# Eleven modulation vectors of a diffusion backbone: from scalar-times-column sums closed on TensorE to one fused multiply-and-sum per output tile on VectorE

## The chip, the cores and the metric

The kernel runs on one core of one Trainium2 chip, in float32 throughout. The metric is the device time of one launch in microseconds; three runs of the kernel before gave 1650.07, 1650.58 and 1651.04 us, so 1650.58 us is the median. One further execution was profiled.

## The reference

The reference is one inference step of a four-layer backbone over 128 context tokens and 256 latent tokens (384 columns in all) of width 1024. The two groups of tokens have different conditioning vectors, `c_ctx` and `c`. Each layer draws six modulation vectors of 1024 numbers from each condition:

```python
mod = jax.nn.silu(cond) @ p['w_mod'][i] + p['b_mod'][i]
sh1, sc1, g1, sh2, sc2, g2 = jnp.split(mod[:, None, :], 6, axis=-1)
h = x * (1 + sc1) + sh1
out = lru_mixer(h) or short_conv_mixer(h) or pool_mixer(h)      # by layer
x = layer_norm(ALPHA * x + g1 * out, ln_g[i, 0], ln_b[i, 0])
h = x * (1 + sc2) + sh2
f = squared_relu_mlp(h, w1, b1, w2, b2)                         # width 4096 inside
x = layer_norm(ALPHA * x + g2 * f, ln_g[i, 1], ln_b[i, 1])
```

So there are 4 x 6 modulation vectors, each a product of a 1024 x 1024 slice of `w_mod` with two condition vectors. Layers 0 and 3 have the recurrent mixer (LRU), layer 1 the short convolution, layer 2 the pooling.

## The kernel before, in words

**Layout.** Activations lie transposed: eight tiles `X0` to `X7` of 128 channels by 384 columns stay in SBUF for the whole run. A linear layer is cut into 128 x 128 weight tiles. Weights come from HBM in transfers of 16 tiles (1 MB, tile `raw`, four buffers). ScalarE copies 8 tiles (a half, 128 x 1024) to `whi` in the float32r type (L1289), and VectorE writes the remainder to `wlo` (L1295); `whi` and `wlo` have four buffers each (`W_BUFS`), and a half is split three halves ahead of its use (`LEAD`). TensorE then makes three products per weight tile, hi x hi, lo x hi and hi x lo (L197 to L199). One weight tile is one tick of a counter by which later work is deferred (`defer`, `tick`).

**The program's order.** The lines of the kernel trace instructions in one order; the framework then lists them anew, engine by engine, by its own idea of what is ready, and each engine works through its list in that order. Waits between engines are on semaphores. `tc.issue_after(x)` holds an instruction behind `x` on the same engine.

**Stages.** LRU of layer 0, its LayerNorm, the MLP of layer 0, its LayerNorm, and so on through four layers. An MLP is 512 weight tiles (64 halves): the first 16 hidden tiles up (`ORD_W1A`), their part of the down product, then the other 16 up and down. Each hidden tile costs VectorE two instructions (L832, L833), each down result two (L547). A LayerNorm after a mixer lets VectorE and GpSimd subtract a shift (L570) and gather sums of x and of its squares (`s1t` on GpSimd L594 and L597, `s2t` on VectorE L595 and L598 in the LRU layers), while TensorE still works on the last output tiles; then TensorE forms the means (L619 to L622).

**The modulation vectors.** The first two of layer 0 have a path of their own. Eleven (`ORD_MOD_PE`) are matrix-vector products on TensorE (`gemv`, L351). The other eleven (`ORD_MOD_DVE`) are made by VectorE during the MLPs of layers 0, 1 and 2, four, three and four of them, in `mac` (L426). For each of them:

- Four transfers of 1 MB bring the weights, with input channels on the partitions; the two buffers are a part of the scratch tile `scr` (shown as `mac`) and a tile `xs` of the same pool (shown as `macr`).
- VectorE multiplies a 128 x 512 piece by a per-partition scalar from `sil` and adds it to a 128 x 512 sum: 4 instructions of L444 (the first piece) and 28 of L446 per vector, for 2 halves of the output, 2 conditions and 8 input tiles. In all 44 and 308.
- The sum over partitions is closed on TensorE: `close` (L448) issues 8 small matmuls per half of a vector with the 0/1 columns `pick` as weights (L453), 22 times in all; then VectorE transposes the result from PSUM (L381) and adds the bias (L384). `finish` lets GpSimd form the combined scales from the vector.

The instructions of `mac` are deferred to ticks after the start of the MLP, spread by `step`.

Of the kernel before, what the change touches and what calls it, by code (L numbers as in the profile page):

```python
# [123 lines left out]
NSCR = 12 * LB  # L124
# [6 lines left out]
def backbone_kernel(ctx, tc, xT, par, wmod0, wmodp, wmodv, w1, w2, lin, lgate, lout, scin, scout, poolw, y_out, st_out):  # L131
# [132 lines left out]
    pick = cst(64, "pick")  # L264
# [160 lines left out]

    def mac(vecs, first, step):  # L426
        t = scr.tile([P, NSCR], F32, tag="scr", name=nm("mac"))
        raw = [t[:, :2048], scr.tile([P, 6 * LB], F32, tag="xs", name=nm("macr"))]
# [8 lines left out]
        def one(i, q, k):
            a = sums[i // 2 % 2][k]
            x = raw[i % 2][:, 512 * q : 512 * q + 512]
            c = 4 * (i % 2) + q  # L440
            w = sil[:, c, k : k + 1]
            with tc.issue_after(hcur["end"].ins):
                if c == 0:
                    vec.tensor_scalar(a, x, w, None, op0=ALU.mult)  # L444
                else:
                    vec.scalar_tensor_tensor(a, x, w, a, op0=ALU.mult, op1=ALU.add)  # L446

        def close(i):  # L448
            (l, v), h, _ = blocks[i]
            ps = acc()  # L450
            for k in range(2):
                for j in range(4):
                    pe.matmul(  # L453
                        ps[32 * j : 32 * j + 32, :P],
                        lhsT=pick[:, 32 * k : 32 * k + 32],
                        rhs=sums[i // 2 % 2][k][:, P * j : P * j + P],
                        start=(k == 0),
                        stop=(k == 1),
                        tile_position=(0, 32 * j),
                    )  # L460
# [918 lines left out]
def _layout(i):  # L1379
# [61 lines left out]
_INS = ["xT", "par", "wmod0", "wmodp", "wmodv", "w1", "w2", "lin", "lgate", "lout", "scin", "scout", "poolw"]  # L1441
# [30 lines left out]
```

## Time and profile before

| what | value |
|---|---|
| runs, median of three | 1650.58 us (1650.07 to 1651.04) |
| profiled execution, its own time | 1649.62 us |
| span of its trace | 1647.8 us |
| mean granted TensorE clock | 0.989 |
| TensorE busy | 1583.4 us (96%) |
| VectorE busy | 1188.8 us (72%) |
| ScalarE, GpSimd busy | 749.8 us (46%), 362.7 us (22%) |
| moved by DMA | 287.75 MB, 175 GB/s |

In the rows of the profile an instruction is given by its line, engine, operation and tiles (out<-in, with buffer numbers left out), then the count, the busy time and the mean duration of one, and the time that its engine sat idle before it with what ended that. A busy time of TensorE is not time at its peak, since matmuls are pipelined; starts tell more than durations there. The three MLPs in which `mac` works lie at about 190 to 450, 590 to 860 and 950 to 1220 us.

### The profile page before, as it was taken

To read this page: it belongs to the slowest core of one execution; us is meant where nothing else is said; L and a number is where in the kernel's file an instruction comes from. 1 tells how busy PE (TensorE), PEld (TensorE's weight loads), DVE (VectorE), ACT (ScalarE), POOL (GpSimd) and SP (SyncE) were. 2 spreads that over 40 slices of the span, in tenths; PEclk is the share of its full clock that TensorE was granted. 3 is DMA by queue.
4 is the path that set the end of the run, shared out by engine and by line. 5 is a ranking of instruction groups with operands and counts; after the bars stand their busy time and mean duration, and the time that the engine had idled before them with its cause. 6 is when DMAs were issued, how large, how long until landed. Compare 5 with 4: busy or idle time off the path is not lost.

```text
span 1647.8 us, 24431 instructions
## 1 busy us (share of the span) xinstructions
PE 1583.4 (96%) x9656; PEld 1501.8 (91%) x9656; DVE 1188.8 (72%) x1822; ACT 749.8 (46%) x1130; POOL 362.7 (22%) x445
## 2 busy tenths in 40 slices
PE   6999999999999999999997899999999999999996
PEld 5778899999999999999996599999988889999995
DVE  4789998886475569867746899688467997434544
ACT  3796642343253345324424553244259947423432
POOL 2114440002320146000055360000541134000043
PEclk9999999999999999999998999999999999999998
DMA  9677456556443535654543256546423344333321
GB/s 358 253 282 268 141 207 244 201 189 237 140 155 124 200 133 205 230 178 159 223 157 128 103 205 244 202 171 226 154 90 119 143 160 144 124 123 123 128 77 38
DMA packets 42162, 287.75 MB, mean 175 GB/s; under 512 B 4800, under 2 KB 6976, under 8 KB 8128
## 3 DMA queue, kind: packets, MB, share of 16 engines
q1 hardware_dynamic: 42048, 286.20, 48.4%
q8 instruction: 75, 1.23, 0.3%
q14 instruction: 39, 0.32, 0.1%
HBM read 284.59 MB, written 1.59 MB: 174 GB/s over the span
## 4 chain that ended last, share of the span: by engine, by line
PE 80%; DVE 12%; ACT 4%; issue 2%; POOL 1%; DMA 1%; SPq 0%; DVEq 0%; POOLq 0%; ACTq 0%
PE acc L197 26%; PE acc L199 25%; PE acc L198 25%; DVE wlo L1295 2%; DVE lru L879 1%; DMA raw<-in_wmod 1%; ACT hidf L930 1%; PE acc L453 1%; DVE X L570 1%; DVE hidf L958 1%; DVE X L547 1%; ACT L933 1%; ACT hidf L933 1%; DVE X L659 1%; POOL h L723 1%
## 5 line engine op out<-in xcount | busy, mean ns | idle before, releaser
L1295 DVE TENSOR_TENSOR wlo<-raw,whi 128x1024 fp32r<-128x1024 f32 x338 | 433.7, 1284 | 168.0 <-ACT whi L1289 166.7
L1289 ACT ACTIVATE whi<-raw 128x1024 fp32r<-128x1024 f32 x338 | 356.1, 1056 | 428.1 <-PE acc L199 351.7
L197 PE MATMUL acc<-h,whi 128*128 128x384 f32 (+2 forms) x1488 | 507.6, 341 | 16.0 <-ACT h L718 10.5
L198 PE MATMUL acc<-h,wlo 128*128 128x384 f32 (+2 forms) x1488 | 504.5, 339 | 0.0
L199 PE MATMUL acc<-h,whi 128*128 128x384 f32 (+2 forms) x1488 | 476.5, 340 | 3.1 <-POOL h L723 3.1
L197 PE MATMUL acc<-hid,whi 128*128 128x384 f32 (+1 forms) x1216 | 412.8, 340 | 0.8 <-ACT hid L975 0.8
L199 PE MATMUL acc<-hid,whi 128*128 128x384 f32 (+1 forms) x1216 | 409.4, 337 | 0.9 <-DVE hid L979 0.9
L198 PE MATMUL acc<-hid,wlo 128*128 128x384 f32 (+1 forms) x1216 | 409.2, 336 | 0.0
L197 PEld LDWEIGHTS acc<-h,whi 128*128 128x128 f32 x1488 | 280.9, 189 | 26.5 <-ACT h L718 11.6
L199 PEld LDWEIGHTS acc<-h,whi 128*128 128x128 f32 x1488 | 277.5, 188 | 6.7 <-POOL h L723 5.5
L198 PEld LDWEIGHTS acc<-h,wlo 128*128 128x128 f32 x1488 | 280.7, 189 | 1.6 <-issue 0.5
L197 PEld LDWEIGHTS acc<-hid,whi 128*128 128x128 f32 x1216 | 228.3, 188 | 5.2 <-issue 2.8
L199 PEld LDWEIGHTS acc<-hid,whi 128*128 128x128 f32 x1216 | 228.4, 188 | 1.5 <-DVE hid L979 1.5
L198 PEld LDWEIGHTS acc<-hid,wlo 128*128 128x128 f32 x1216 | 228.3, 188 | 0.9
L830 ACT ACTIVATE tmp<-acc,par 128x384 f32<-128x384 f32 x128 | 74.3, 580 | 259.1 <-PE acc L199 259.1
L570 POOL TENSOR_TENSOR X<-X,ssb 128x384 f32<-128x384 f32 x49 | 55.6, 1169 | 483.8 <-ACT ssb L568 483.8
L547 DVE SCALAR_TENSOR_TENSOR X<-acc,m,X 128x128 f32<-128x128 f32 (+1 forms) x176 | 64.7, 412 | 125.5 <-PE acc L199 123.7
L446 DVE SCALAR_TENSOR_TENSOR mac<-macr,sil,mac 128x512 f32<-128x512 f32 x176 | 126.2, 754 | 0.0
L832 DVE TENSOR_TENSOR tmp<-tmp 128x384 f32<-128x384 f32 x128 | 72.2, 564 | 65.8 <-ACT tmp L830 65.7
L446 DVE SCALAR_TENSOR_TENSOR mac<-mac,sil 128x512 f32<-128x512 f32 x132 | 95.2, 759 | 0.0
L777 POOL TENSOR_SCALAR X<-X,ag,xbb 128x128 f32<-128x128 f32 x64 | 94.8, 1495 | 0.4
L420 POOL TENSOR_SCALAR sc<-m 128x16 f32<-128x16 f32 x7 | 2.8, 403 | 328.6 <-DVE m L384 328.2
(194 smaller groups left out, 1310.6 us busy)
## 6 DMA issues: line engine op xcount, KB each, us to landing
raw<-in_w SPq DMA_DIRECT2D x128, 1024.0 KB, 4.8
raw<-in_wmodp SPq DMA_DIRECT2D x26, 1024.0 KB, 4.9
macr<-in_wmodv SPq DMA_DIRECT2D x22, 1024.0 KB, 5.3
mac<-in_wmodv SPq DMA_DIRECT2D x22, 1024.0 KB, 4.8
park<-in_wmodp SPq DMA_DIRECT2D x18, 1024.0 KB, 8.2
raw<-in_lin SPq DMA_DIRECT2D x16, 1024.0 KB, 5.1
raw<-in_scin SPq DMA_DIRECT2D x12, 1024.0 KB, 4.8
raw<-in_wmod SPq DMA_DIRECT2D x8, 1024.0 KB, 7.7
```

Of the source, the lines that this page charges most:

```text
L197: pe.matmul(ps, lhsT=hi, rhs=xhi, start=first, stop=False)
L198: pe.matmul(ps, lhsT=lo, rhs=xhi, start=False, stop=False)
L199: late = lambda: pe.matmul(ps, lhsT=hi, rhs=xlo, start=False, stop=last)
L446: vec.scalar_tensor_tensor(a, x, w, a, op0=ALU.mult, op1=ALU.add)
L547: vec.scalar_tensor_tensor(Xt[c][:, o : o + n], ps[:, a:b], col(g, c, k), Xt[c][:, o : o + n], op0=ALU.mult, op1=ALU.add)
L570: (vec if fast and i > 2 else gp).tensor_tensor(Xt[i], Xt[i], ssb, op=ALU.subtract)
L777: gp.tensor_scalar(Xt[c][:, a:b], Xt[c][:, a:b], col(g, c, k), col(xb, c, k), op0=ALU.mult, op1=ALU.add)
L830: act.activation(r, ps[:, :T], AF.Relu, bias=par_t[:, i : i + 1])
L832: vec.tensor_tensor(q, r, r, op=ALU.mult)
L933: act.activation(S["tau", c], S["tau", c], AF.Sqrt, scale=0.25)
L1289: act.activation(hi, raws[id(raw)][:, i * 1024 : (i + 1) * 1024], AF.Copy)
L1295: vec.tensor_tensor(lo, raws[id(raw)][:, i * 1024 : (i + 1) * 1024], hi.bitcast(F32), op=ALU.subtract)
```

## The change

The weights of the eleven vectors are laid out the other way round in HBM: an output channel on each partition, the 1024 input channels along the row. A block is now 128 partitions x two rows of 1024 (two output tiles), 1 MB as before, four blocks to a vector. One VectorE instruction multiplies a 128 x 1024 row block by a row of the condition, broadcast to all partitions (`silb`), and sums along the row into one column (`accum_out`): 4 per block, 16 per vector, 176 in all. The products are written to a scratch area `prod` that nobody reads. `close` only adds the bias to the 128 x 16 result, without TensorE; `pick`, the closing matmuls, the transposes and the `xs` buffer are gone (both weight buffers lie in `scr` now).

The row `silb` (128 x 2048: 1024 numbers for each of the two conditions) is made once, by a new function that is traced behind the LayerNorm of layer 0's mixer: a 1 MB transfer, a ScalarE tanh, and two VectorE instructions, all 128 x 2048. The arithmetic of the vectors is otherwise the same.

```diff
-NSCR = 12 * LB
+NSCR = 5 * D
...
+    def setup_rows(crow):
+        nc.sync.dma_start(silb, crow)
+        t = scr.tile([P, NSCR], F32, tag="scr", name=nm("sb"))[:, : 2 * D]
+        act.activation(t, silb, AF.Tanh, scale=0.5)
+        vec.tensor_scalar(t, t, 1.0, 0.5, op0=ALU.add, op1=ALU.mult)
+        vec.tensor_tensor(silb, t, silb, op=ALU.mult)
...
     def mac(vecs, first, step):
         t = scr.tile([P, NSCR], F32, tag="scr", name=nm("mac"))
-        raw = [t[:, :2048], scr.tile([P, 6 * LB], F32, tag="xs", name=nm("macr"))]
+        raw = [t[:, : 2 * D], t[:, 2 * D : 4 * D]]
+        prod = t[:, 4 * D : 5 * D]
...
             with tc.issue_after(hcur["end"].ins):
-                if c == 0:
-                    vec.tensor_scalar(a, x, w, None, op0=ALU.mult)
-                else:
-                    vec.scalar_tensor_tensor(a, x, w, a, op0=ALU.mult, op1=ALU.add)
+                vec.scalar_tensor_tensor(
+                    prod,
+                    raw[i % 2][:, D * q : D * q + D],
+                    1.0,
+                    silb[:, D * k : D * k + D],
+                    op0=ALU.mult,
+                    op1=ALU.mult,
+                    accum_out=rows[l, v][:, o : o + 1],
+                )
...
         def close(i):
-            (l, v), h, _ = blocks[i]
-            ps = acc()
-            for k in range(2):
-                for j in range(4):
-                    pe.matmul(
-                        ps[32 * j : 32 * j + 32, :P],
-                        lhsT=pick[:, 32 * k : 32 * k + 32],
-                        rhs=sums[i // 2 % 2][k][:, P * j : P * j + P],
...
-            collect(l, v, ps[:, :P], 4 * h)
-            if h == 1:
-                finish(l, v)
+            l, v = blocks[i][0]
+            m = modT[l, v] = rows[l, v]
+            o = PCOLS["bmod"][0] + (l * 6 + v) * 2 * C
+            vec.tensor_tensor(m, m, par_t[:, o : o + 2 * C], op=ALU.add)
+            finish(l, v)
...
     ln_tail(1, to_h(1, "mm"), use)
+    X(lambda: setup_rows(crow))
     use = mlp(0, ORD_MOD_DVE[0])
```

The change moves instructions in three places. Line numbers of the changed kernel are 2 to 3 higher from L549 on, and tile numbers differ because one constant tile is gone (`X_100` before is `X_99` now, both the fourth tile of x).

The first place is TensorE's list in the MLP of layer 0, where the first half vector is closed. Before:

```order
L197 MATMUL acc_2294<-h_1781,whi_2181 128x384
L198 MATMUL acc_2294<-h_1781,wlo_2182 128x384
L199 MATMUL acc_2294<-h_1781,whi_2181 128x384
L453 MATMUL acc_2318<-mac_1846,pick 32x128 x8
L197 MATMUL acc_2294<-h_1781,whi_2181 128x384
```

Now:

```order
L198 MATMUL acc_2287<-h_1778,wlo_2179 128x384
L199 MATMUL acc_2287<-h_1778,whi_2178 128x384
L197 MATMUL acc_2287<-h_1778,whi_2178 128x384
L198 MATMUL acc_2287<-h_1778,wlo_2179 128x384
L199 MATMUL acc_2287<-h_1778,whi_2178 128x384
```

The 22 groups of eight closing matmuls have left the list; every other matmul of the program stands in the order that it had.

The second place is VectorE's list in the LayerNorm of layer 0's mixer (`s2t` is the sum of squares, `X` the residual tiles as they take up the mixer's output). Before:

```order
L595 TENSOR_TENSOR s2t<-tmp_1563,tmp_1591 128x384
L1295 TENSOR_TENSOR wlo_1608<-raw_1341,whi_1607 128x1024
L598 TENSOR_TENSOR s2t<-s2t,tmp_1603 128x384
L547 SCALAR_TENSOR_TENSOR X_100<-acc_1491,m_857,X_100 128x128
L547 SCALAR_TENSOR_TENSOR X_100<-acc_1491,m_857,X_100 128x256
L1295 TENSOR_TENSOR wlo_1643<-raw_1341,whi_1642 128x1024
```

Now:

```order
L597 TENSOR_TENSOR s2t<-tmp_1560,tmp_1588 128x384
L1298 TENSOR_TENSOR wlo_1605<-raw_1338,whi_1604 128x1024
L600 TENSOR_TENSOR s2t<-s2t,tmp_1600 128x384
L429 TENSOR_TENSOR silb<-sb_1844,silb 128x2048
L549 SCALAR_TENSOR_TENSOR X_99<-acc_1488,m_854,X_99 128x128
L549 SCALAR_TENSOR_TENSOR X_99<-acc_1488,m_854,X_99 128x256
```

The second instruction of the `silb` setup has come in ahead of the fourth tile's residual. The first one (L428, 128 x 2048) stands 14 rows higher, behind the residual of the first tile and ahead of a `wlo`; on ScalarE the tanh stands right ahead of the `whi` of that same half.

The third place is VectorE's list in the MLP of layer 0, while the hidden tiles come up (`wlo` is a weight split, L832 and L833, now L834 and L835, finish a hidden tile). Before:

```order
L1295 TENSOR_TENSOR wlo_2223<-raw_1930,whi_2222 128x1024
L833 TENSOR_TENSOR hid_2209<-tmp_2208,hid_2209 128x384
L444 TENSOR_SCALAR mac_1846<-mac_1846,sil 128x512 x2
L446 SCALAR_TENSOR_TENSOR mac_1846<-mac_1846,sil 128x512
L832 TENSOR_TENSOR tmp_2246<-tmp_2245 128x384
L446 SCALAR_TENSOR_TENSOR mac_1846<-mac_1846,sil 128x512
L1295 TENSOR_TENSOR wlo_2261<-raw_1930,whi_2260 128x1024
```

Now:

```order
L1298 TENSOR_TENSOR wlo_2218<-raw_1931,whi_2217 128x1024
L450 SCALAR_TENSOR_TENSOR mac_1848,m_2005<-mac_1848,silb 128x1024
L834 TENSOR_TENSOR tmp_2241<-tmp_2240 128x384
L450 SCALAR_TENSOR_TENSOR mac_1848,m_2005<-mac_1848,silb 128x1024
L835 TENSOR_TENSOR hid_2242<-tmp_2241,hid_2242 128x384
L1298 TENSOR_TENSOR wlo_2255<-raw_1931,whi_2254 128x1024
L450 SCALAR_TENSOR_TENSOR mac_1848,m_2005<-mac_1848,silb 128x1024
```

Between two weight splits there stood three to four instructions of 512 elements, and now stand two of 1024. In the whole list 20 of the new instructions stand within the 12 splits of this stretch, 32 within the next 15 (the down product) and 12 within the 6 after that; before, 37 of the old ones stood within the first 12, and the last one came some 13 splits later than now. Of the 176 new instructions 50 stand right behind another one.

More of the change, by code (lines that the diff above doesn't have):

```diff
@@ L263, in backbone_kernel @@
     ssb = cst(T, "ssb")
-    pick = cst(64, "pick")
     Xt = [cst(T, f"X{c}") for c in range(C)]
@@ L293, in setup_params @@
         )
-        gp.memset(pick, 0.0)
-        gp.memset(pick[:, 0:1], 1.0)
-        gp.memset(pick[:, 33:34], 1.0)
         gp.memset(ones_s, 1.0 / P)
@@ L424, in finish @@
             comb["h", 2 * l + h] = (gg, bb)
+    silb = cst(2 * D, "silb")
+    def setup_rows(crow):
[4 more added lines that the diff above has]
+        vec.tensor_tensor(silb, t, silb, op=ALU.mult)
     def mac(vecs, first, step):
         t = scr.tile([P, NSCR], F32, tag="scr", name=nm("mac"))
-        raw = [t[:, :2048], scr.tile([P, 6 * LB], F32, tag="xs", name=nm("macr"))]
@@ L429, in mac @@
-        sums = [[t[:, 2048 + 1024 * i + 512 * k : 2560 + 1024 * i + 512 * k] for k in range(2)] for i in range(2)]
-        blocks = [(v, h, b) for v in vecs for h in range(2) for b in range(2)]
+        raw = [t[:, : 2 * D], t[:, 2 * D : 4 * D]]
+        prod = t[:, 4 * D : 5 * D]
+        blocks = [(v, b) for v in vecs for b in range(4)]
+        rows = {}
         def fetch(i):
             if i < len(blocks):
-                v, h, b = blocks[i]
-                nc.sync.dma_start(raw[i % 2][:, :2048], wmodv[MOD_DVE[v], h, b])
+                v, b = blocks[i]
+                nc.sync.dma_start(raw[i % 2], wmodv[MOD_DVE[v], b])
@@ L437, in one @@
         def one(i, q, k):
[L438 to L441, printed above, removed]
+            (l, v), b = blocks[i]
+            if (l, v) not in rows:
+                rows[l, v] = const.tile([P, 2 * C], F32, tag=f"m{l % 2}{v}", name=f"m{l}{v}")
+            o = 2 * (2 * b + q) + k
             with tc.issue_after(hcur["end"].ins):
-                if c == 0:
-                    vec.tensor_scalar(a, x, w, None, op0=ALU.mult)
-                else:
-                    vec.scalar_tensor_tensor(a, x, w, a, op0=ALU.mult, op1=ALU.add)
@@ L468, in mac @@
         for i in range(len(blocks)):
-            for q in range(4):
+            for q in range(2):
                 for k in range(2):
-                    defer(at(8 * i + 2 * q + k), lambda a=(i, q, k): one(*a))
+                    defer(at(8 * i + 4 * q + 2 * k), lambda a=(i, q, k): one(*a))
             defer(at(8 * i + 8) + 2, lambda i=i: fetch(i + 2))
-            if i % 2 == 1:
-                defer(at(8 * i + 8) + 10, lambda i=i: close(i))
+            if i % 4 == 3:
+                defer(at(8 * i + 8) + 4, lambda i=i: close(i))
     first_mod = const.tile([P, 32], F32, tag="m00", name="m00")
@@ L1417, in _layout @@
     r["wmodp"] = np.stack(wp).reshape(len(wp), 4, P, 2048)
-    wv = [wm[l, :, :, s].reshape(2, 4, P, 2, 4, 4, 32).transpose(3, 0, 2, 1, 5, 4, 6) for l, s in sum(ORD_MOD_DVE, [])]
-    r["wmodv"] = np.stack(wv).reshape(len(wv), 2, 2, P, 2048)
+    wt = a["w_mod"].reshape(DEPTH, D, 6, 4, 2, P)
+    wv = [wt[l, :, s].transpose(1, 3, 2, 0) for l, s in sum(ORD_MOD_DVE, [])]
+    r["wmodv"] = np.stack(wv).reshape(len(wv), 4, P, 2 * D)
+    crow = np.concatenate([a["c_ctx"], a["c"][0]])
+    r["crow"] = np.ascontiguousarray(np.broadcast_to(crow, (P, 2 * D)))
     w0 = wm[0, :, :, :2].reshape(2, 4, P, 2, 4, 2, 4, 32).transpose(4, 0, 2, 1, 6, 3, 5, 7)
@@ L1438, in _layout @@
     return r
[L1441 removed]
+_INS = ["xT", "par", "crow", "wmod0", "wmodp", "wmodv", "w1", "w2", "lin", "lgate", "lout", "scin", "scout", "poolw"]
 def _build(arrays):
```

6 lines of the change are left out of this document (1 added, 5 removed).

## The prediction

> **What bounds the kernel now.** I read the profile from the top: the engines' shares, then the chain that ended last, then the three MLPs, where the edited code works.
>
> ```profile
> PE 1583.4 (96%) x9656; PEld 1501.8 (91%) x9656; DVE 1188.8 (72%) x1822; ACT 749.8 (46%) x1130; POOL 362.7 (22%) x445
> PE 80%; DVE 12%; ACT 4%; issue 2%; POOL 1%; DMA 1%; SPq 0%; DVEq 0%; POOLq 0%; ACTq 0%
> ```
>
> TensorE (PE) carries 80% of the chain, VectorE (DVE) 12%. The windows of the three MLPs, in columns PE, PEld, DVE, ACT, POOL, clock, DMA share and GB/s:
>
> ```profile
> 190.00:450.00 260.00, 260.00 (x1580) 256.00 (x1580) 206.61 (x309) 100.75 (x143) 53.98 (x47) 1.00 0.57 203
> 590.00:860.00 270.00, 269.60 (x1658) 263.18 (x1657) 198.53 (x298) 108.38 (x160) 57.41 (x45) 1.00 0.51 183
> 950.00:1220.00 270.00, 269.14 (x1669) 262.17 (x1668) 208.00 (x311) 98.16 (x139) 56.96 (x71) 1.00 0.53 189
> ```
>
> PE never pauses there, at a granted clock of 1.00: whatever leaves its list shortens the run. But DVE is not far off. The same view in steps of 20 us:
>
> ```profile
> 210.00:230.00 20.00, 20.00 (x116) 20.00 (x115) 20.00 (x29) 9.57 (x15) 12.67 (x8) 1.00 0.60 211
> 250.00:270.00 20.00, 20.00 (x128) 19.55 (x127) 20.00 (x34) 6.15 (x7) 0.00 (x0) 1.00 0.63 225
> 270.00:290.00 20.00, 20.00 (x128) 19.55 (x127) 13.81 (x23) 5.31 (x5) 0.00 (x0) 1.00 0.71 250
> ```
>
> For some 75 us DVE is full as well and only just keeps pace. So two questions decide: what PE gets rid of, and whether DVE still keeps pace with the new instructions.
>
> **What PE loses.** The instructions of the closing line, and the chain of waits around the first close:
>
> ```profile
> L453 PE MATMUL acc<-mac,pick x352: 272/273/297, 231.2 to 1187.4; 128*32 128x128 f32 x176
> 231.13 0.17 PE acc L199
> 231.30 0.57 PE acc L453 x16
> 231.87 0.37 PE acc L197
> 232.24 0.17 PE acc L198
> ```
>
> Sixteen records make a close, 352 make 22. A close holds the chain for 0.57 us, and the matmul behind it for 0.37 instead of some 0.175 (0.17 or 0.18 in these rows), 0.195 more: 0.765 us together. All 22 lie in the MLPs, from 231.2 to 1187.4 us. The term is 22 x 0.765 = **-16.8 us**. Its lower bound is 22 x 0.57 = -12.5, were the pause behind a close an artefact of modelled ends.
>
> **What DVE has instead.** The groups by shape (busy us, mean ns) and a stretch of its timeline in the full phase:
>
> ```profile
> L446 DVE SCALAR_TENSOR_TENSOR mac<-macr,sil,mac 128x512 f32<-128x512 f32 x176 | 126.2, 754 | 0.0
> L446 DVE SCALAR_TENSOR_TENSOR mac<-mac,sil 128x512 f32<-128x512 f32 x132 | 95.2, 759 | 0.0
> L916 DVE SCALAR_TENSOR_TENSOR hidf<-hidf,lru 128x776 f32<-128x776 f32 x12 | 11.5, 961 | 3.4 <-ACT hidf L895 3.4
> L936 DVE TENSOR_TENSOR hidf<-hidf,hidf 128x776 f32<-128x776 f32 x10 | 9.4, 962 | 7.6 <-ACT hidf L933 7.6
> 252.82 0.56 DVE L832 TENSOR_TENSOR tmp<-tmp 128x384 f32<-128x384 f32 x1
> 253.29 1.22 DVE L1295 TENSOR_TENSOR wlo<-raw,whi 128x1024 fp32r<-128x1024 f32 x1
> 254.43 0.56 DVE L833 TENSOR_TENSOR hid<-tmp,hid 128x384 fp32r<-128x384 f32 x1
> 254.90 2.74 DVE L446 SCALAR_TENSOR_TENSOR mac<-macr,sil,mac 128x512 f32<-128x512 f32 x4
> 257.55 1.23 DVE L1295 TENSOR_TENSOR wlo<-raw,whi 128x1024 fp32r<-128x1024 f32 x1
> 258.68 2.08 DVE L446 SCALAR_TENSOR_TENSOR mac<-macr,sil,mac 128x512 f32<-128x512 f32 x3
> 260.67 0.74 DVE L547 SCALAR_TENSOR_TENSOR X<-acc,m,X 128x128 f32<-128x128 f32 x2
> 261.32 1.22 DVE L1295 TENSOR_TENSOR wlo<-raw,whi 128x1024 fp32r<-128x1024 f32 x1
> ```
>
> From start to start a split (`wlo`) takes 1.14 us, a hidden tile's instruction 0.47, a residual pair 0.65, an old sum 2.65/4 = 0.66. A scalar_tensor_tensor with an immediate scalar runs like a tensor_tensor (961 and 962 ns at 776 elements), so the new instruction over 1024 elements takes 1.14 us, as the split does. What is open is the sum that it must write out; no instruction of before does that. The nearest rows:
>
> ```profile
> 51.81 0.18 DVE L325 TENSOR_TENSOR sp<-sp 128x32 f32<-128x32 f32 x1
> 51.91 1.22 DVE L1295 TENSOR_TENSOR wlo<-raw,whi 128x1024 fp32r<-128x1024 f32 x1
> 48.38 1.33 DVE L319 SCALAR_TENSOR_TENSOR sp<-sp,sp 128x32 f32<-128x32 f32 x6
> ```
>
> A small instruction between others takes 0.10 us, one that depends on its forerunner 1.33/6 = 0.22. Lower bound: no time of its own, 1.14 in all. Upper: it starts when the duration of 1.22 has ended and takes a small one's 0.17, 1.39. I take 1.24 (the 0.10 row: its neighbours are other work), and 0.14 more, up to that upper end's 1.39, for the 50 of 176 that stand right behind another and wait for it: **1.28 us** on average, written t. In all, DVE then gives 176 x 1.28 = 225 us where it gave about 308 x 0.66 = 203 for L446, besides L444 and the transposes: little more work, but denser.
>
> [...]
>
> **Does DVE keep pace?** PE needs 24 x 0.175 = 4.2 us for a half of 8 weight tiles. Counting the MLP of layer 0 by its list in three stretches of 12, 15 and 6 splits, with 20, 32 and 12 new instructions:
> - 12 x 1.14 + 16 hidden tiles x 0.94 + 20t = 28.7 + 20t, against 50.4 us of PE
> - 15 x 1.14 + 7.5 residual pairs x 0.65 + 32t = 22.0 + 32t, against 63.0
> - 6 x (1.14 + 0.94) + 12t = 12.5 + 12t, against 25.2
>
> DVE falls behind by 64t - 75.4 us. How far may it? A split has four buffers, so ScalarE can start one (L1289) only as PE finishes the half four earlier, which is when it starts the half three earlier:
>
> ```profile
> 250.44 1.05 ACT L1289 ACTIVATE whi<-raw 128x1024 fp32r<-128x1024 f32 x1
> 263.31 1.06 ACT L1289 ACTIVATE whi<-raw 128x1024 fp32r<-128x1024 f32 x1 [3.92 <-PE acc L199]
> ```
>
> The half whose `whi` began at 250.44 is used from 263.31, the start of the third split after it; its `wlo` ended at 253.29 + 1.22 = 254.51. Cushion: 8.8 us. Before, 37 old sums stood in the first stretch: 28.7 + 37 x 0.66 = 53.1 against 50.4 + 0.8 for a close, so 1.9 us of it had gone already. The full cushion is 10.7, and PE waits only for t above (75.4 + 10.7)/64 = **1.35 us**. At 1.28 the lag is 6.5 and costs nothing; at 1.39 it is 2.9 over in each of the MLPs of layers 0 and 2. In layer 1, with 48 instructions in 25 splits by the same count, 48t - 57.3 - 10.7 is negative up to 1.41. Term: **0, up to +5.8**.
>
> **What the setup adds.** In the LayerNorm of layer 0's mixer DVE is full, and here PE does wait:
>
> ```profile
> 155.20 1.21 DVE L1295 TENSOR_TENSOR wlo<-raw,whi 128x1024 fp32r<-128x1024 f32 x1
> 156.87 4.90 DVE L570 TENSOR_TENSOR X<-X,ssb 128x384 f32<-128x384 f32 x5 [0.46 <-ACT ssb L568]
> 163.92 2.04 DVE L1295 TENSOR_TENSOR wlo<-raw,whi 128x1024 fp32r<-128x1024 f32 x1
> 166.35 0.73 DVE L547 SCALAR_TENSOR_TENSOR X<-acc,m,X 128x128 f32<-128x128 f32 x2
> 174.10 0.91 PE L619 MATMUL acc<-s1t,ones_m 128*128 128x384 f32 x2 [1.88 <-POOL s1t L597]
> ```
>
> The first DVE instruction of the setup (128 x 2048, one input) comes ahead of the 155.20 split; the old L444 took 483 ns for 512 by its group, so 1.3 (if fixed time is shared) to 1.9 us. The tanh on ScalarE, two splits' worth (2 x 1.06 at most), delays that split's `whi` by as much; 0.46 us of DVE idle hides a part. The subtractions behind it run beside GpSimd's (L570 at 0.98 each against 0.47 alone), so a later start wins some back: I take +0.3. The second (128 x 2048, two inputs) costs 2 x 1.07 + 0.07 = 2.2 us ahead of the 166.35 residual; the last sums of squares then come 2 to 2.5 us later. Some of that returns, since the shared last steps (sum, then residual of `X7`) overlap otherwise: **+2.0 us**, bounds 0.5 and 5 (all three at full length, nothing hidden). The transfer of `silb` takes the place that the first `macr` transfer had in SP's queue, 1 MB for 1 MB. The first transfer of `mac` now waits for the second setup instruction, and the weight transfer behind it for a split that is listed later still; it is needed only some 20 us on. GpSimd loses three small memsets, worth nothing.
>
> **Sum.** 1649.6 (profiled execution; the median of the runs is 1.0 higher) - 16.8 + 0 + 2.0 = 1634.8, on the scale of the runs up to 1635.8. I predict **1635.5 us**. Its own range: 1632 (no setup cost, 1649.6 - 16.8 = 1632.8, rounded out) to 1645 (the closes at -12.5 instead of -16.8 add 4.3 and the setup at 5 adds 3.0: 1642.8; with a part of the lag's 5.8).
>
> **Rivals.**
> - *The sum runs at half rate* (slower). With two fp32 inputs and a sum to keep, an element might take two steps: of the 1.14 us, 1.07 go with the elements (0.67 us between 384 and 1024 of them) and 0.07 are fixed, so t = 2 x 1.07 + 0.07 + 0.10 = 2.31. Lag over cushion: 64 x 2.31 - 86.1 = 62 us in two MLPs, 48 x 2.31 - 68.0 = 43 in one: 1635 + 167 = 1802 us. Against it: the same operation without a sum shows nothing of it (961 beside 962 ns). It decides from t = 1.35. [...] Chance 0.06.
> - *The write-out is dearer than any row says.* At t = 1.45 the MLPs lose 6.7 + 6.7 + 1.6 = 15 us: 1650, no change; at 1.5 some 24: 1659. For it: the chain of semaphores between neighbours; against: the 0.10 row. Chance 0.12.
> - *The setup stalls the LayerNorm* more than its lengths say (ScalarE and GpSimd queue behind it): +8 instead of 2, 1641. Chance 0.06.
> - *The closes were hidden*, and PE would have waited for weights or VectorE at those places: no change, 1650. Against it: no PE wait in the windows. Chance 0.04.
>
> **How the numbers follow.** The forecast has 0.72. A change of 0.2%, 3.3 us, is about what a measurement can tell here. Faster: 0.72 + 0.06 (setup) + 0.05 of the dear write-out = 0.83. Same: 0.04 + 0.04 of the write-out = 0.08. Slower: 0.06 + 0.03 = 0.09. Left out of 1632 to 1645 are the half rate, the hidden closes and most of the write-out, some 0.2.
>
> **What would show it.** In the profile after: no L453; PE without waits at L197 to L199 in the MLPs; L450 at 1.22 us, followed in 0.1 us or so by whatever reads the sum; a `wlo` that ends at least 3 us before its use; PE's wait ahead of the means at some 176 instead of 174.1 us. Wrong: PE idle in the MLPs with `wlo` as releaser, or L450 above 1.4 us.

## The result, and the profile after

| kernel | runs, median (us) | ratio to before, 95% interval |
|---|---|---|
| before | 1650.32 (1649.49 to 1651.04) | |
| changed | 1637.54 (1636.94 to 1638.17) | 0.9924 (0.9912 to 0.9936) |

The changed kernel is 12.8 us faster. 1635.5 us was predicted, 2.0 less than came. The profiled execution took 1636.94 us with a span of 1635.2, which is 12.6 less than before's span.

The shares of the engines on the page:

```profile
PE 1568.7 (96%) x9304; PEld 1496.4 (92%) x9304; DVE 1169.3 (72%) x1791; ACT 751.8 (46%) x1131; POOL 400.6 (24%) x442
```

The windows of the three MLPs, with the columns as before:

```profile
190.00:450.00 260.00, 260.00 (x1489) 259.63 (x1488) 203.65 (x303) 104.66 (x150) 72.45 (x51) 1.00 0.57 204
590.00:860.00 270.00, 269.60 (x1588) 265.87 (x1587) 194.49 (x290) 109.94 (x162) 72.77 (x47) 1.00 0.52 187
950.00:1220.00 270.00, 268.74 (x1574) 265.28 (x1573) 206.25 (x315) 106.97 (x157) 62.53 (x71) 1.00 0.52 185
```

TensorE is as full in the MLPs as it was, with the 352 records of the closes gone; the weight loads (second number) no longer have the gaps that the closes tore (259.63 of 260 against 256.00). VectorE stays full for longer, as windows of 20 us of the same kernel show:

```profile
250.00:270.00 20.00, 20.00 (x117) 20.00 (x116) 19.90 (x32) 6.10 (x8) 0.00 (x0) 1.00 0.78 266
310.00:330.00 20.00, 20.00 (x116) 20.00 (x115) 19.86 (x32) 7.08 (x9) 0.00 (x0) 1.00 0.77 278
330.00:350.00 20.00, 20.00 (x117) 20.00 (x116) 15.81 (x25) 8.99 (x14) 1.69 (x3) 1.00 0.64 232
```

Before, it had room again from 270 us; now only after 330. TensorE has 20.00 of 20 throughout.

The new instruction as a group (busy us, mean ns, idle time ahead):

```profile
L450 DVE SCALAR_TENSOR_TENSOR mac<-mac,silb 128x1024 f32<-128x1024 f32 x176 | 216.1, 1228 | 1.7
```

What it costs VectorE is read from its timeline, by starts (first number) more than by durations (second):

```profile
240.99 1.21 DVE L450 SCALAR_TENSOR_TENSOR mac<-mac,silb 128x1024 f32<-128x1024 f32 x1
242.14 0.08 DVE L450 DVE_READ_ACCUMULATOR mac<-mac,silb 128x1 f32 x1
242.25 1.23 DVE L450 SCALAR_TENSOR_TENSOR mac<-mac,silb 128x1024 f32<-128x1024 f32 x1
246.74 1.23 DVE L450 SCALAR_TENSOR_TENSOR mac<-mac,silb 128x1024 f32<-128x1024 f32 x1
247.89 0.08 DVE L450 DVE_READ_ACCUMULATOR mac<-mac,silb 128x1 f32 x1
247.89 0.56 DVE L834 TENSOR_TENSOR tmp<-tmp 128x384 f32<-128x384 f32 x1
257.56 1.22 DVE L1298 TENSOR_TENSOR wlo<-raw,whi 128x1024 fp32r<-128x1024 f32 x1
258.69 1.22 DVE L450 SCALAR_TENSOR_TENSOR mac<-mac,silb 128x1024 f32<-128x1024 f32 x1
```

The write-out of the sum is an instruction of its own (`DVE_READ_ACCUMULATOR`). Where another kind of instruction follows, that one starts at the same hundredth as the write-out: 246.74 to 247.89 is 1.15 us from start to start, as a split takes 1.13 (257.56 to 258.69). Where another of the new instructions follows, it starts 0.11 after the write-out: 240.99 to 242.25 is 1.26, and all 50 such pairs take 1.25 to 1.28. So t is 1.15 for 126 of the 176 and 1.26 for 50, 1.18 on average, not 1.28.

The LayerNorm of layer 0's mixer is where time was lost. TensorE's first pair of matmuls for the means:

```profile
175.85 1.65 PE L621 MATMUL acc<-s1t,ones_m 128*128 128x384 f32 x2 [5.13 <-POOL s1t L599]
```

The windows behind it, with the granted clock as the third number from the end:

```profile
176.00:178.00 2.00, 2.00 (x4) 1.09 (x5) 0.87 (x3) 0.52 (x1) 0.00 (x0) 0.50 1.01 422
178.00:180.00 2.00, 2.00 (x6) 0.99 (x4) 0.00 (x0) 0.35 (x1) 0.00 (x0) 0.74 0.49 201
```

TensorE waits 5.13 us for `s1t` where it waited 1.88 (GpSimd forms `s1t`, and in the chain of waits its last steps start behind VectorE's residuals, L549), and then works at a granted clock of 0.50, so that the pair of L621 takes 1.65 us instead of 0.91. Ahead of it VectorE has the setup in its timeline:

```profile
154.06 1.23 DVE L428 TENSOR_SCALAR sb<-sb 128x2048 f32<-128x2048 f32 x1 [0.25 <-ACT sb L427]
155.20 1.22 DVE L1298 TENSOR_TENSOR wlo<-raw,whi 128x1024 fp32r<-128x1024 f32 x1
156.34 4.89 DVE L572 TENSOR_TENSOR X<-X,ssb 128x384 f32<-128x384 f32 x5
165.81 2.28 DVE L429 TENSOR_TENSOR silb<-sb,silb 128x2048 f32<-128x2048 f32 x1
168.01 1.38 DVE L549 SCALAR_TENSOR_TENSOR X<-acc,m,X 128x128 f32<-128x128 f32 x4
```

**Where the 12.6 us went.** Spans carry some noise from the start: TensorE's first matmul started at 8.32 us here, and between 7.9 and 10.2 in the profiles of the experiments, each time behind a transfer of weights.

```profile
8.32 1.93 PE L489 MATMUL acc<-raw,sil 128*32 128x128 f32 x32 [8.32 <-DMA raw<-in_wmod]
```

So stages are compared by the starts of the means' matmuls (L619 before, L621 now) in TensorE's timeline, from one LayerNorm to another:

| stage, from means to means | before | changed | difference |
|---|---|---|---|
| start to the first means (layer 0's mixer) | 174.10 | 175.85 | +1.75 |
| MLP of layer 0 (with the rest of that LayerNorm) | 282.89 | 278.12 | -4.77 |
| mixer of layer 1 | 142.89 | 142.95 | +0.06 |
| MLP of layer 1 | 281.59 | 276.94 | -4.65 |
| mixer and MLP of layer 2 | 331.34 | 326.35 | -4.99 |
| all behind, to the end of the span | 435.0 | 435.0 | 0 |

The MLP of layer 1 had six closes: 0.775 us each. From the first means' start to the first matrix-vector products was 2.78 us before and is 4.34 now, by the lower clock; without these 1.56 the MLP of layer 0 has lost 6.33 us, 0.79 for each of eight closes. The first row is 3.25 us of longer wait, less 1.4 of an earlier start and 0.1 of small parts.

### The profile page after: what moved, and what is told of

Its sections match the earlier page's. It is cut to its first block, busy times and chain, and to the rows that moved or that the text cites. A ratio compares the mean times of both kernels' runs of the same rounds, so it can differ in the third digit from the quotient of the medians.

```text
span 1635.2 us, 23710 instructions
## 1 busy us (share of the span) xinstructions
PE 1568.7 (96%) x9304; PEld 1496.4 (92%) x9304; DVE 1169.3 (72%) x1791; ACT 751.8 (46%) x1131; POOL 400.6 (24%) x442
## 4 chain that ended last, share of the span: by engine, by line
PE 79%; DVE 12%; ACT 5%; issue 2%; POOL 1%; DMA 1%; SPq 0%; DVEq 0%; POOLq 0%; ACTq 0%
PE acc L199 26%; PE acc L198 26%; PE acc L197 25%; DVE wlo L1298 2%; DVE lru L881 1%; ACT hidf L932 1%; DMA raw<-in_wmod 1%; DVE hidf L960 1%; DVE X L549 1%; DVE X L572 1%; ACT L935 1%; ACT hidf L935 1%; DVE X L661 1%; DVE hidf L949 1%; POOL h L725 1%
## 5 line engine op out<-in xcount | busy, mean ns | idle before, releaser
L450 DVE SCALAR_TENSOR_TENSOR mac<-mac,silb 128x1024 f32<-128x1024 f32 x176 | 216.1, 1228 | 1.7
L832 ACT ACTIVATE tmp<-acc,par 128x384 f32<-128x384 f32 x128 | 74.2, 580 | 248.1 <-PE acc L199 248.1
L572 POOL TENSOR_TENSOR X<-X,ssb 128x384 f32<-128x384 f32 x49 | 56.1, 1179 | 488.7 <-ACT ssb L570 488.7
L834 DVE TENSOR_TENSOR tmp<-tmp 128x384 f32<-128x384 f32 x128 | 73.3, 572 | 104.2 <-ACT tmp L832 104.2
L549 DVE SCALAR_TENSOR_TENSOR X<-acc,m,X 128x128 f32<-128x128 f32 (+1 forms) x176 | 64.7, 411 | 113.9 <-PE acc L199 112.0
L779 POOL TENSOR_SCALAR X<-X,ag,xbb 128x128 f32<-128x128 f32 x64 | 126.9, 1997 | 0.4
L416 POOL TENSOR_SCALAR sc<-m 128x16 f32<-128x16 f32 x7 | 6.4, 911 | 270.8 <-DVE m L464 269.4
L835 DVE TENSOR_TENSOR hid<-tmp,hid 128x384 fp32r<-128x384 f32 x128 | 72.3, 565 | 0.3
```

Of the source, the lines that this page charges most:

```text
L450: vec.scalar_tensor_tensor(prod, raw[i % 2][:, D * q : D * q + D], 1.0, silb[:, D * k : D * k + D], op0=ALU.mult, op1=ALU.mult, accum_out= ...
L549: vec.scalar_tensor_tensor(Xt[c][:, o : o + n], ps[:, a:b], col(g, c, k), Xt[c][:, o : o + n], op0=ALU.mult, op1=ALU.add)
L572: (vec if fast and i > 2 else gp).tensor_tensor(Xt[i], Xt[i], ssb, op=ALU.subtract)
L779: gp.tensor_scalar(Xt[c][:, a:b], Xt[c][:, a:b], col(g, c, k), col(xb, c, k), op0=ALU.mult, op1=ALU.add)
L832: act.activation(r, ps[:, :T], AF.Relu, bias=par_t[:, i : i + 1])
L834: vec.tensor_tensor(q, r, r, op=ALU.mult)
```

## The experiments

All have the changed kernel or the kernel before as their base and were timed in five rounds. An undisturbed MLP of layer 0, at a full clock in its LayerNorm, takes 276.5 us from means to means in these traces; that is the measure for waits in it.

### The setup alone, in the kernel before

```diff
     ln_tail(1, to_h(1, "mm"), use)
+    X(lambda: setup_rows(crow))
```

> The kernel before, with the silb transfer and its three instructions added at the same place as in the changed kernel and silb left unused; everything else as before. Theory (the setup costs the LayerNorm 4.8 us, whatever the rest of the change does): 1650.3 + 4.8 = 1655.1 us, TensorE's wait ahead of the means about 5.1 us and a granted clock near 0.5 behind it. Prediction's term: 1652.3 us. Rival (the stall in the changed kernel comes from something else): 1650.3 us.

Measured: 1655.59 us, ratio 1.0034 (1.0021 to 1.0046), 5.4 us slower than the kernel before, timed beside it. TensorE's rows for the means:

```profile
177.02 1.65 PE L619 MATMUL acc<-s1t,ones_m 128*128 128x384 f32 x2 [5.13 <-POOL s1t L597]
178.46 1.49 PE L620 MATMUL acc<-s2t,ones_m 128*128 128x384 f32 x2
```

The same wait, to the hundredth, and the lower clock, with nothing else of the change in place. The setup costs 5 us here, not 2.

### The closes back, in the changed kernel

```diff
+    def idle_close():
+        ps = acc()
+        for k, j in [(k, j) for k in range(2) for j in range(4)]: pe.matmul(ps[32 * j : 32 * j + 32, :P], lhsT=ones_m[:, 32 * k : 32 * k + 32], rhs=ones_m, ...)
...
+            if i % 2 == 1: defer(at(8 * i + 8) + 10, idle_close)
```

> The changed kernel, with 22 groups of eight matmuls of the closing shape (128 x 32 weights, 128 columns, two passes over four row groups) put back on TensorE at the ticks of the old closes; they read a constant and nobody reads them, so they wait for no VectorE sum. Theory (each close held TensorE for 0.77 us by its own length and the pause behind it, and VectorE's new work costs nothing): 1637.5 + 17 = 1654.5 us. If the pause behind a close is an artefact of modelled ends: 1637.5 + 12.5 = 1650. Rival (the closes were dear because they waited for VectorE's sums, or because VectorE's lighter list made the rest run better): clearly below 1650.

Measured: 1655.29 us, ratio 1.0033 (1.0020 to 1.0045), 17.8 us more than the changed kernel. A group of the eight, in TensorE's timeline:

```profile
235.66 0.33 PE L199 MATMUL acc<-h,whi 128*128 128x384 f32 x1
235.92 0.65 PE L161 MATMUL acc<-ones_m 128*32 128x128 f32 x16
236.49 0.44 PE L197 MATMUL acc<-h,whi 128*128 128x384 f32 x1
236.77 0.33 PE L198 MATMUL acc<-h,wlo 128*128 128x384 f32 x1
```

0.57 us and a pause behind it, as in the closes of before, although these wait for no sum. The MLP of layer 1 takes 281.59 us from means to means, exactly what it took before. So the closes' price is TensorE's own, the pause behind them is real, and VectorE's new work costs the MLPs nothing. The rival of closes that were dear through their waits falls.

### The setup behind the LayerNorm

```diff
-        act.activation(t, silb, AF.Tanh, scale=0.5)
-        vec.tensor_scalar(t, t, 1.0, 0.5, op0=ALU.add, op1=ALU.mult)
-        vec.tensor_tensor(silb, t, silb, op=ALU.mult)
+        with tc.issue_after(hcur["mark_a"].ins): act.activation(t, silb, AF.Tanh, scale=0.5)
+        with tc.issue_after(hcur["end"].ins):
+            vec.tensor_scalar(t, t, 1.0, 0.5, op0=ALU.add, op1=ALU.mult)
+            vec.tensor_tensor(silb, t, silb, op=ALU.mult)
```

> The changed kernel, with the three instructions that make silb held behind the LayerNorm of layer 0's mixer (tanh behind the third tile's hi copy, the two VectorE instructions behind the tail's last one) instead of in its middle. Theory (the setup in the middle of the LayerNorm costs 4.8 us: 3.25 of longer TensorE wait ahead of the means, 5.13 against 1.88, and 1.6 of lower granted clock after it): about 1637.5 - 4.8 = 1632.7 us, TensorE's wait ahead of the means back at about 1.9 us, granted clock 1.00 at 172 to 180 us. Prediction's own term (2.0): 1635.5 us. Rival (the 4.8 us were the late start of something else, a transfer or the order of the residuals, and not the setup): 1637.5 us as now. If the setup only moves its cost into the start of the MLP (first splits late): also about 1637, but with a TensorE wait for wlo at 190 to 200 us.

Measured: 1635.41 us, ratio 0.9910 (0.9895 to 0.9925). The wait for the means and two later rows of TensorE:

```profile
173.86 0.91 PE L621 MATMUL acc<-s1t,ones_m 128*128 128x384 f32 x2 [1.91 <-POOL s1t L599]
191.68 0.44 PE L197 MATMUL acc<-h,whi 128*128 128x384 f32 x1 [1.57 <-ACT h L720]
197.51 0.97 PE L198 MATMUL acc<-h,wlo 128*128 128x384 f32 x4 [0.44 <-DVE wlo L1298]
```

ScalarE's timeline ahead of the first of those two:

```profile
188.01 1.28 ACT L427 ACT_TABLE_LOAD   x1
189.30 1.91 ACT L427 ACTIVATE sb<-silb 128x2048 f32<-128x2048 f32 x1
191.12 0.51 ACT L720 ACTIVATE h<-tmp 128x384 fp32r<-128x384 f32 x1
```

All of the 4.8 us in the LayerNorm come back (a wait of 1.91, the clock at 1.00), but more than half is lost again: the tanh needs a load of function tables here, 1.28 us, which it did not need beside the mixer, and the two hold up a copy of `h` that TensorE waits for. From means to means the MLP of layer 0 takes 279.34 us, 2.8 more than undisturbed. The theory on the LayerNorm holds; that the setup would be free right behind it does not, and the expected 1632.7 did not come.

### Only the second instruction behind the LayerNorm

```diff
-        vec.tensor_tensor(silb, t, silb, op=ALU.mult)
+        with tc.issue_after(hcur["end"].ins):
+            vec.tensor_tensor(silb, t, silb, op=ALU.mult)
```

> The changed kernel, with only the second VectorE instruction of the silb setup (2.28 us, two inputs) held behind the LayerNorm of layer 0's mixer; the tanh and the first VectorE instruction stay in it. It shows which of the two made TensorE's wait ahead of the means 3.25 us longer. By the prediction's two terms (the first +0.3, the second +1.7): the wait falls from 5.13 to about 2.2 us, with the clock at 1.00 behind it, and the run to about 1633.5 us (3 us of wait and 1.6 of clock less, perhaps 0.5 given back at the start of the MLP). Rival (the first and the tanh in front of it, ahead of the shift of the tiles, cost most): the wait stays above 4 us and the run at about 1637.

Measured: 1634.74 us, ratio 0.9910 (0.9896 to 0.9923). TensorE's rows for the means:

```profile
174.50 0.91 PE L621 MATMUL acc<-s1t,ones_m 128*128 128x384 f32 x2 [2.81 <-POOL s1t L599]
175.25 0.85 PE L622 MATMUL acc<-s2t,ones_m 128*128 128x384 f32 x2
175.90 1.49 PE L623 MATMUL acc<-X,ones_m 128*128 128x384 f32 x2
```

The second instruction was worth 5.13 - 2.81 = 2.32 us of wait, its whole length; the tanh and the first are worth 2.81 - 1.88 = 0.93. The clock fell all the same, in the middle of the four pairs (the third takes 1.49 us, 0.81 before), which was not expected behind a wait of 2.81.

### TensorE kept busy in its wait

```diff
+            if idx == 1: es = ExitStack(); es.enter_context(tc.issue_after(lastmm[0].ins)); [pe.matmul(m2[:, :P], lhsT=ones_m, rhs=ones_m, start=True, stop=True) for _ in range(NWARM)]; es.close()
```

(`NWARM` is 24; `lastmm` is the last product of the mixer.)

> The changed kernel, with 24 matmuls of 128 x 128 constants put on TensorE between the last output matmul of layer 0's mixer and the matmuls that form its means, in the place where TensorE now waits 5.1 us; their results are overwritten. Theory (the lower granted clock after that wait, 0.50 and 0.74, comes from the idle time and costs 1.6 us by itself): about 1636 us, the clock 1.00 at 176 to 180 us, the means still waiting for s1t at the same time. Rival (the clock falls there for another reason, or the 1.6 us are not on the path): 1637.5 us or a little more, with the lower clock still there.

Measured: 1636.60 us (1634.11 to 1638.87), ratio 0.9919 (0.9905 to 0.9932). TensorE's timeline, with the added matmuls (L620):

```profile
169.63 5.52 PE L620 MATMUL acc<-ones_m 128*128 128x128 f32 x48
174.99 0.84 PE L621 MATMUL acc<-s1t,ones_m 128*128 128x384 f32 x2
175.66 0.81 PE L622 MATMUL acc<-s2t,ones_m 128*128 128x384 f32 x2
```

The clock stays at 1.00 and the stage from the means through the MLP takes 276.47 us instead of 278.12. In this trace the lower clock went with the idle time; the runs alone, 0.9 us apart with wide spreads, would not show it.

### The setup in halves, among the first tiles of the MLP

```diff
+    def setup_half(p, s):
+        with tc.issue_after(hcur["last_a"].ins): act.activation(p, s, AF.Tanh, scale=0.5)
+        with tc.issue_after(hcur["end"].ins):
+            vec.tensor_scalar(p, p, 1.0, 0.5, op0=ALU.add, op1=ALU.mult)
+            vec.tensor_tensor(s, p, s, op=ALU.mult)
...
+        for k in range(2 if vecs is ORD_MOD_DVE[0] else 0): defer(10 + 8 * k, lambda k=k: setup_half(prod, silb[:, D * k : D * k + D]))
```

> The changed kernel, with the silb setup cut into two halves of 1024 (one per condition) that use the product area as scratch and stand behind the LayerNorm, among the first weight tiles of the MLP of layer 0, where VectorE is not full. Theory (the setup costs nothing where VectorE and ScalarE have room): TensorE's wait ahead of the means 1.9 us, none above 0.5 us in the first 20 us of the MLP, about 1632.7 us, 2.7 less than the version that held the whole setup right behind the LayerNorm (1635.4, with waits of 1.57 for h and 0.44 for wlo at 191 to 198 us). Rival (the tanh behind the LayerNorm costs ScalarE a change of function tables, so h or the hidden tiles come late again): 1634 to 1636 us with waits for ScalarE at 185 to 205 us.

Measured: 1633.10 us (1631.45 to 1634.71), ratio 0.9897 (0.9883 to 0.9910), the best median. TensorE waits 1.88 us for the means and nowhere for the setup; the load of tables (1.28 us, at 196.09) falls where ScalarE has room. But here too the clock fell, to 0.50, behind a wait of only 1.88:

```profile
173.40 0.91 PE L621 MATMUL acc<-s1t,ones_m 128*128 128x384 f32 x2 [1.88 <-POOL s1t L599]
174.15 0.95 PE L622 MATMUL acc<-s2t,ones_m 128*128 128x384 f32 x2
174.90 1.48 PE L623 MATMUL acc<-X,ones_m 128*128 128x384 f32 x2
```

### The same, with TensorE kept busy in the wait that is left

The two edits together, with `NWARM` 8.

> The version with the silb setup in halves in the MLP (1633.1 us), with 8 matmuls of constants (0.23 us each, 1.84 us) in TensorE's remaining wait of 1.88 us ahead of the means. Its profile had a granted clock of 0.50 behind that wait, which cost 1.4 us between the means and the matrix-vector products (4.19 us against 2.78). If the idle time brings the lower clock: 1.00 throughout, 1632 us. If the lower clock comes from elsewhere: 1633, with the clock still down.

Measured: 1633.25 us (1632.64 to 1633.49), ratio 0.9898 (0.9884 to 0.9912). In the profile the clock is 1.00 at this place and the MLP of layer 0 takes 276.57 us from means to means, against 277.98 in the version without. The medians are the same. What the trace shows at one place, 1.4 us, is within the scatter of the runs. Behind the same wait of 1.88 us the kernel before kept its clock at 1.00, so the version without need not have the fall in every execution; the last section shows what decides it.

### Longer new instructions, freely ordered

```diff
-NSCR = 5 * D
+NSCR = 5 * D + 512; EXT = 512
...
-                    raw[i % 2][:, D * q : D * q + D],
+                    raw[i % 2][:, D * q - EXT * q : D * q + D + EXT * (1 - q)],
```

> The changed kernel, with each of the 176 new instructions running over 1280 elements instead of 1024 (the sums take in 256 products too many), so that from start to start one takes about 1.15 + 256 x 1.07/1024 = 1.42 us. By the prediction's cushion (TensorE waits from t = 1.35; lag 64t - 86.1 in the MLPs of layers 0 and 2, 48t - 68.0 in layer 1): 4.8 + 4.8 + 0.2 = +9.8, 1647.3 us, with TensorE waits for wlo in the MLPs. Rival (the cushion is larger, since VectorE's list can be rearranged and the lag is made up between the stretches): 1637.5 us, no such waits.

> The same with 1536 elements (512 too many): t about 1.15 + 512 x 1.07/1024 = 1.69 us. By the prediction's cushion: 64 x 1.69 - 86.1 = 22 in each of two MLPs and 48 x 1.69 - 68.0 = 13 in one, +57, so 1695 us. Rival (larger cushion): if 256 costs nothing, then clearly less than 57; the difference between the two lengths gives the slope (64 + 64 + 48 instructions by 0.27 us = 47 us once VectorE sets the pace).

Measured: 1639.21 us (ratio 0.9934, 0.9921 to 0.9946) and 1637.59 us (0.9929, 0.9916 to 0.9941): nothing beyond 1.7 us, which is within the scatter, where 10 and 57 us had been expected. The instructions are as long as meant, here in the group of those with 1536 elements:

```profile
L450 DVE SCALAR_TENSOR_TENSOR mac<-mac,silb 128x1536 f32<-128x1536 f32 x176 | 309.4, 1758 | 0.8
```

VectorE is full until 390 us in that kernel, and TensorE is full beside it, as its windows show:

```profile
350.00:370.00 20.00, 20.00 (x116) 20.00 (x116) 20.00 (x29) 8.71 (x15) 0.00 (x0) 1.00 0.68 245
370.00:390.00 20.00, 20.00 (x116) 20.00 (x115) 20.00 (x29) 8.81 (x14) 0.00 (x0) 1.00 0.61 220
```

The reason stands in VectorE's list. The 64 new instructions of the first MLP span 32 weight splits in the changed kernel, 40 at 1280 elements and 47 at 1536. The framework that lists the instructions anew thus goes by their lengths: the longer they are, the fewer it puts between two splits. The prediction's lag was counted on a fixed list.

### The same instructions, packed into 32 splits

To hold the list fixed, two of them are put between each two splits in the MLPs of layers 0 and 2, 32 times, and a split is held behind those ahead of it. In layer 1, with 48 of them, the list was not fixed: they still span 24, 29 and 31 splits at the three lengths.

```diff
-            X(lambda: mac(todo, 32, 13.2 / len(todo)))
+            X(lambda: mac(todo, 32, 8.0 / len(todo)))
...
-        with after("mark_v"):
+        with after("mark_v"), after("stt"):
```

> The changed kernel, with the new instructions packed into the first 32 weight splits after the start of an MLP: exactly two between two splits in the MLPs of layers 0 and 2 (three in two gaps in layer 1), each split held behind the instructions ahead of it. Instructions as they are (1024 elements, t = 1.15). By the prediction's way of counting (12 splits of the up product with 16 hidden tiles, 16 of the down product, 4 up again) VectorE falls behind by 24t - 21.7 = 5.9 us in the first part and makes it up in the second, under the cushion of 10.7: no TensorE wait, 1637.5 us. Rival (there is hardly a cushion; the changed kernel is only fast because its list was spread to what VectorE can do): TensorE waits for wlo in the first part, up to 6 us in each MLP, up to 1650.

> The same packing with 1280 elements (sums with 256 products too many), t = 1.42 us. Lag by the prediction's counting: 24t - 21.7 = 12.4, then 32t - 43.8 = 1.6, then 8t - 8.5 = 2.9: 16.9 in all, 6.2 over the cushion of 10.7 in each of the MLPs of layers 0 and 2, nothing in layer 1: 1637.5 + 12.4 = 1650 us, with TensorE waits for wlo. Without a cushion 34 us: 1671. Rival (the order never matters, VectorE always catches up): 1637.5.

> The same packing with 1536 elements (512 products too many), t = 1.69 us. Lag by the prediction's counting: 18.9 + 10.3 + 5.0 = 34.2 us, 23.5 over the cushion in two MLPs, nothing in layer 1: 1637.5 + 47 = 1684 us. The freely ordered kernel with the same instructions took 1637.6, so what is over that is due to the order alone. Rival (order of no matter): 1637.5.

| elements | run (us) | ratio | MLP of layer 0 | of layer 1 | mixer and MLP of layer 2 |
|---|---|---|---|---|---|
| 1024 | 1638.97 | 0.9934 (0.9921 to 0.9946) | +0.5 | 0 | -0.3 |
| 1280 | 1655.92 | 1.0036 (1.0023 to 1.0049) | +9.3 | 0 | +8.0 |
| 1536 | 1694.40 | 1.0267 (1.0253 to 1.0281) | +26.7 | +2.1 | +26.4 |

The last three columns are the stages from means to means, against 276.5, 276.94 and 325.4 us (the last as in the freely ordered kernel with 1280 elements), those of layer 0 without the lower clock in its LayerNorm. The two longer ones came 6 and 10 us above what was expected, so the rival of an order that never matters falls. At 1536 elements the same work costs 57 us more than in a free order. A window of that kernel:

```profile
250.00:270.00 20.00, 15.71 (x85) 14.65 (x86) 20.00 (x27) 8.07 (x12) 1.25 (x1) 1.00 0.53 174
```

One of TensorE's waits in it:

```profile
251.04 0.44 PE L198 MATMUL acc<-h,wlo 128*128 128x384 f32 x1 [1.22 <-DVE wlo L1298]
```

VectorE is full and TensorE at 15.71 of 20. The count of the prediction holds once the list is fixed: from 1280 to 1536 elements the MLP of layer 0 grows by 17.5 us, 64 instructions by 0.27. But the cushion is smaller than 10.7: the count gives a lag of 64 x 1.41 - 74.0 = 16.2 us at 1280 elements, of which 9.3 and 8.0 were paid, so 6.9 and 8.2 were free; at 1536 it is 64 x 1.68 - 74.0 = 33.5, less 26.7 and 26.4, so about 7. (1.41 and 1.68 us are the starts' distances in VectorE's timelines, as 1.15 is for 1024 elements.)

## Why the prediction was right

**The closes (-16.8): right.** The stages give 6.33 us for the eight of layer 0 and 4.65 for the six of layer 1; for the eight of layer 2 it is 5.9, with the 325.4 us that the stage takes in most profiles without closes (331.34 before). That is 16.9 for all 22. Putting them back cost 17.8. The pause behind a close was no artefact of modelled ends, so the lower bound of 12.5 was out.

**The new instruction (t = 1.28): too high, on the safe side.** It is 1.15, near the lower bound of 1.14, where other work follows, and 1.26 where another new one does; 1.18 on average. The read of the sum takes 0.08 us as a row and, before other work, nothing from start to start. So the estimate of 0.10 for a small instruction priced something that is hidden, while the 0.14 more for the 50 neighbours was near the 0.11 that they take. The rivals of half rate (2.31) and of a dear write-out (1.45) fall with it: no run shows either. The accumulating form on two fp32 inputs takes 1.15 us from start to start at 1024 elements where other work follows, beside 1.13 for the split, which keeps no sum.

**Does VectorE keep pace (0): right, by a weaker argument than it looked.** A `wlo` of the full phase, and the `whi` of the third split after it:

```profile
257.56 1.22 DVE L1298 TENSOR_TENSOR wlo<-raw,whi 128x1024 fp32r<-128x1024 f32 x1
265.05 1.06 ACT L1292 ACTIVATE whi<-raw 128x1024 fp32r<-128x1024 f32 x1 [3.13 <-PE acc L199]
```

It belongs to the `whi` that began at 252.98, three splits ahead of the one at 265.05, so by the prediction's way of reading 6.3 us were left (265.05 less 258.78), the least in the stretch with the new instructions; at least 3 had been said. The threshold, though, failed twice. With a cushion of 7 to 8 us instead of 10.7 it lies near (75.4 + 7.3)/64 = 1.29, so at the t that was assumed TensorE would have been on the edge. And for an instruction whose length the listing takes into account nothing was lost up to 1.68 us: it moves the rest behind later splits. A bound of 5.8 us for a t of 1.39 was thus worth nothing. At the t of 1.18 that was run, the count gives a lag of 0.1 us (64 x 1.18 - 75.4), so the cushion was not put to the test. A length that the listing does not know was not tried.

**The setup (+2.0): the failed step.** It costs 3.25 us of wait and 1.56 of clock, 4.8 us in this execution, at the end of its bounds (0.5 to 5). Three things went wrong in the term:
- "a later start wins some back: I take +0.3" for the tanh and the first instruction. They cost 0.93. VectorE spends 1.14 on L428 from start to start and waits 0.25 ahead of it, where it had waited 0.46 ahead of the subtractions: 1.14 + 0.25 - 0.46 = 0.93. The five L572 take 4.89 us as before (4.90): nothing is won back.
- "Some of that returns" for the second. It took 2.20 us (165.81 to 168.01), and removing it took 2.32 off the wait. Where VectorE is full and TensorE's wait hangs on the end of its list, an instruction cost its length here.
- The clock was not in the sum. Behind the longer wait TensorE ran at a granted clock of 0.50 from 176 to 178 us and of 0.74 from 178 to 180, which cost the 1.56.

The length of a wait alone does not say whether the clock falls behind it. In all eight profiles with a wait of 5.1 us it fell to 0.50; where such a wait was filled with matmuls, and where one of 1.88 us was, it stayed at 1.00 (one profile each); behind unfilled waits of 1.88 to 2.81 us it fell in two of four. What the falls have in common in these traces is in the last section.

One of the signs that the prediction named, the means "at some 176 instead of 174.1 us", was met at 175.85 by luck: the wait grew by 3.25 us, and this execution started 1.4 earlier.

**The sum.** 1649.6 - 16.9 (closes) + 4.8 (setup) = 1637.5, and 1636.94 was run. What is left are an earlier start (-1.4) and 1.0 us more in the stage of layer 2 than in most other profiles of this kernel's kin (326.35 against 325.1 to 325.5), where the clock was at 0.50 for 3.4 us more (from 930 us on) than in those. So the forecast was 2 us low for one reason, the setup, which was 2.8 us dearer than its term.

## What to carry to other kernels

An instruction that was added off the bottleneck was free here only in a stretch where its engine had room: the same three instructions cost 4.8 us in a LayerNorm whose chain runs through VectorE, 2.8 right behind it, and, cut into halves, nothing some 10 us later among the tiles of an MLP; and a function that changes ScalarE's tables has to be counted with the load, 1.28 us here. Where a framework orders the lists, the room is spread by it, and a lag that is counted on one list says little about another length: the same instructions of 1536 elements were 57 us apart in two orders. Where TensorE is made to wait, look at the granted clock behind the wait as well as at the wait: of the 4.8 us, 1.56 were the clock's.

## What the runs showed of the hardware that was not expected

- The accumulator read has a row of 0.08 us. Where another operation follows it takes no time from start to start; where another accumulating instruction follows it takes 0.11 to 0.12 us: 1.26 instead of 1.15 at 1024 elements (50 pairs), 1.53 instead of 1.41 at 1280 (34), 1.79 instead of 1.68 at 1536 (24).
- In the LayerNorm of layer 3's mixer, where no edit was made, the clock fell behind a wait of some 1.9 us in five of the fourteen profiles, and not in the others. TensorE's row in the kernel with 1536 elements in free order, whose clock was 0.50 from 1340 to 1342 us:

```profile
1339.65 1.34 PE L621 MATMUL acc<-s1t,ones_m 128*128 128x384 f32 x2 [1.87 <-POOL s1t L599]
```

- The granted clock behind a wait of 5.1 us is 0.50 for about 3 us in some executions and for 5 to 6 in others: from the first means to the matrix-vector products it took 4.34 to 5.42 us, against 2.78 at a full clock. Behind waits of some 2 us its fall moves a stage by 1.3 to 1.7 us, in some executions and not in others.
- What decides it can be read from the clock's changes in the fourteen traces. Within a trace all its falls start multiples of 3.41 us apart, on a grid whose place differs from trace to trace. Windows along this grid, with the wait of 1.88 us of the kernel with the setup in halves, and with that of 1.91 of the kernel with the setup behind the LayerNorm (TensorE's busy time is the second number, the clock the third from the end):

```profile
171.28:174.69 3.41, 1.53 (x6) 0.86 (x5) 2.99 (x4) 0.27 (x2) 1.99 (x2) 1.00 0.11 43
174.69:178.10 3.41, 3.41 (x13) 1.28 (x15) 0.33 (x1) 0.78 (x2) 0.00 (x0) 0.50 0.02 5
170.24:173.65 3.41, 1.72 (x10) 1.40 (x8) 3.20 (x6) 1.29 (x3) 3.25 (x3) 1.00 0.53 223
173.65:177.06 3.41, 3.20 (x16) 1.72 (x20) 1.46 (x4) 1.01 (x2) 0.16 (x1) 1.00 0.02 5
```

The first wait lies wholly within one window, which is idle for 1.88 us, and the clock falls at its end. The second is cut by the grid into 1.69 and 0.21, and it stays at 1.00. So it is for all 18 short waits ahead of the means in the LayerNorms of the mixers of layers 0 and 3: the clock fell behind the seven that filled 1.85 us or more of one window, and not behind the eleven that filled 1.84 or less. Behind the waits of 5.1 us, which all fill one window, it stayed low for a second one where the rest of the wait filled 0.90 us or more of that (five profiles), and not where it filled 0.23 or less (three). Over the rest of the traces, with TensorE's idle time in more pieces, the border lies between 1.6 and 2.0 us of a window. No run here moved a wait along the grid by intent, so this is read from the traces alone.

- A change of function tables took ScalarE 1.28 us, in the kernel with the setup behind the LayerNorm (at 188.01 us) and in the one with the setup in halves (at 196.09).
